# Weight sums as whole units with longer rows, and the last of them begun in the value projection and the first u/z run

## The chip, the cores and the metric

The kernel runs on one core of a Trainium2 chip. The metric is the device time of one execution in microseconds (us); lower is better. The core has a matrix engine (PE, TensorE), a vector engine (DVE), a scalar engine (ACT), a general engine (POOL, GpSimd), and a sync engine (SP) that does nothing but issue transfers. Each engine works through its own instructions in order. Transfers issued by SP go over the hardware DMA queue q1, those issued by POOL over the software queue q0; both run on the same 16 DMA engines.

## What is computed

A decoder trunk of two layers over 512 positions with model width 2048, in float32. Cut to what matters here:

```
h = x @ w_in                          # layer 0: attention and gated convolution
y = concat(y_a, y_b) @ w_out          # 2048 x 2048
x = layer_norm(alpha * x + y)
u, v, z = gelu / gelu / linear of x @ od_w_in      # layer 1: three 2048 x 2048 projections
y = (layer_norm(v) mixed over positions) * u * silu(z)
x = layer_norm(alpha * x + y @ od_w_out)           # 2048 x 2048
```

## The kernel before

**Five runs of seven products.** Behind the attention stand five 2048-wide projections, each done as a block-recursive matrix product with seven block products in place of eight: the layer-0 output projection (called the first output run below), the value projection, two u/z runs (r = 0 and r = 1, each half of the columns of u and of z together), and the layer-1 output projection (the last run). `strassen` runs each; its products are numbered p and come in the order 1, 2, 5, 3, 6, 7, 4. A product has two halves c of its depth and two column groups g; for each (p, g, c) it loads two pages of 512 KB of weights, ACT and DVE split each page into a high and a low part (L85, L86), and PE does 24 matmuls on them (L655 to L657), 96 for each product and 672 for a run.

**Where the weights come from.** Products 1, 2 and 3 use blocks of the weight matrix as they are. Products 5, 7, 6 and 4 need sums of blocks. In the two output runs and the value projection, `chained` keeps eight pages `x` in SBUF, loads them once (SP, L593) and lets POOL add a further block into them by an accumulating transfer (L605), once before each of the products 5, 6 and 4; for p = 7 the sum lies ready in DRAM. In the u/z runs all four sums lie ready in DRAM and SP loads them as `raw` pages (`plain`, L577).

**The sums in DRAM.** `weight_sums` makes them, each by three transfers on POOL's queue: a marker of one element that waits for a given tile and so fixes the earliest time of the step (L227), a copy DRAM to DRAM (L229), and an accumulating copy with rows of 1 KB at most (L233, `max_dma_last_dim=1024`). Each sum is done in two halves d of 512 KB. A step holds two sums (two values of g): 2 MB copied and 2 MB accumulated. There are 2 steps for each of the three chained runs and 8 for each u/z run, in the order 5, 5, 7, 7, 6, 6, 4, 4, where the sum for p = 6 is copied from that for p = 7, and that for 4 from that for 6. Their DRAM tiles are named `ts_` (output runs), `tsv_` (value projection) and `tu_` (u/z).

**Where the steps begin.** The loop over the eight heads h of the attention begins those of the first output run, the value projection and both u/z runs, two and a half for each head:

```
for st in early[5 * h // 2:5 * (h + 1) // 2]:
    st(qT[0:1, 0:1])
```

The two steps of the last run begin at the start of u/z run 0, as soon as the tile `swT` is there (L963). A scheduler places every instruction in its engine's order, so the order of the code is not the order on the engine.

**What else stands in the way of the steps.** In the output runs, POOL also adds the residual into the result tile `xv` (L694) after ACT has put a product there (L692), and DVE then takes its statistics (`ready`, L697). In u/z run 0 SP issues, between the raw pages, loads of scale rows (`row`, L862), loads of `xs` (L886) and stores `xres` (L889), for which DVE works at L873, L874, L887 and L888.

Of the kernel before, what the change touches and what calls it, by code (L numbers as in the profile page):

```python
# [10 lines left out]
F32 = mybir.dt.float32  # L11
F32R = mybir.dt.float32r
AF = mybir.ActivationFunctionType
ALU = mybir.AluOpType
AX = mybir.AxisListType

P = 128
# [48 lines left out]
def trunk(ctx, tc, xT, xn, oneh, cst, table, wa, wv, convw, posT, cw1, cw2, wo0, wuz, wv1, odg, odb, sguw, sgub, wo1, out):  # L66
# [128 lines left out]

    def blocks(w):

        def get(k, n, g, c, d):
            return w[4 * (2 * g + n) + 2 * k + c][:, d * 1024:(d + 1) * 1024]
        return get  # L200

    def uz_blocks(r):

        def get(k, n, g, c, d):
            q, e = 2 * r + g, (2 * k + c) * 512 + d * 256
            return wuz[8 * q + n:8 * q + 8:2, :, e:e + 256].rearrange("i p e -> p i e")
        return get

    def same(t, src):
        return t.rearrange("p (i e) -> p i e", i=4) if len(src.shape) == 3 else t  # L210

    GCS = [(g, c) for c in range(2) for g in range(2)]

    def weight_sums(get, qs, name):


        t = {}
        first = {5: (0, 0), 7: (1, 1)}
        more = {5: (0, 1), 7: (0, 1), 6: (0, 0), 4: (1, 0)}

        def step(q, gcs):
            def run(after):

                for g, c in gcs:
                    for d in range(2):
                        h = t[q, g, c, d] = dram.tile([P, 1024], F32, name=f"{name}{q}{g}{c}{d}")
                        nc.gpsimd.dma_start(h[0:1, 0:1], after)  # L227
                        src = get(*first[q], g, c, d) if q in first else t[{6: 7, 4: 6}[q], g, c, d]
                        nc.gpsimd.dma_start(same(h, src), src)  # L229
                for g, c in gcs:  # L230
                    for d in range(2):
                        src = get(*more[q], g, c, d)
                        nc.gpsimd.dma_start(same(t[q, g, c, d], src), src, accum_op=ALU.add, max_dma_last_dim=1024)  # L233
            return run
        return t, [step(q, GCS[i:i + 2]) for q in qs for i in (0, 2)]

# [1 line left out]
    sumsv, stepsv = weight_sums(blocks(wv1), (7,), "tsv_")  # L238
    sums1, steps1 = weight_sums(blocks(wo1), (7,), "ts1_")
    sumsu, stepsu = zip(*(weight_sums(uz_blocks(r), (5, 7, 6, 4), f"tu{r}_") for r in range(2)))  # L240
    early = steps0 + stepsv + stepsu[0] + stepsu[1]


    with ExitStack() as es:
# [229 lines left out]
        for h in range(NH):  # L474
# [20 lines left out]
            if h == 0:  # L495
                cmp_out(1)
            bz = silu2(ps, "bz")
            for st in early[5 * h // 2:5 * (h + 1) // 2]:
                st(qT[0:1, 0:1])
            t0, tc_ = softmax_branch(h, 0, q, bh, bc)  # L500
            compressed(h, tc_)
# [57 lines left out]
    def in_place(a):  # L559
# [12 lines left out]
            return {1: a(0, 0, c), 2: a(0, 1, c), 5: a(1, 0, c), 3: a(0, 1, c), 7: a(1, 0, c), 6: a(0, 0, c), 4: a(1, 1, c)}[p]  # L572
        return src

    def raw_load(src):
        raw = raw_page()
        nc.sync.dma_start(same(raw, src), src)  # L577
        return raw

    def plain(get, sums):  # L580

        def unit(p, g, c, d):
            return raw_load(sums[p, g, c, d] if p in (5, 7, 6, 4) else get(*{1: (0, 0), 2: (1, 0), 3: (1, 1)}[p], g, c, d))
        return unit

    def chained(get, sums, pool, direct):


        x = {}

        def page(g, c, d):
            x[g, c, d] = pool.tile([P, 1024], F32, tag="x", name="x", bufs=8)
            nc.sync.dma_start(x[g, c, d], get(0, 0, g, c, d))  # L593
            return x[g, c, d]

        def unit(p, g, c, d):
            if p == 1 and c not in direct:
                return page(g, c, d)
            if p in (1, 2, 3):
                if p == 2 and c in direct:  # L600
                    page(g, c, d)
                return raw_load(get(*{1: (0, 0), 2: (1, 0), 3: (1, 1)}[p], g, c, d))
            if p == 7:
                return raw_load(sums[p, g, c, d])
            nc.gpsimd.dma_start(x[g, c, d], get(*{5: (0, 1), 6: (1, 1), 4: (1, 0)}[p], g, c, d), accum_op=ALU.add)  # L605
            return x[g, c, d]
        return unit

# [186 lines left out]
    def done_v(p, g, m, b):  # L795
# [8 lines left out]
            nc.scalar.copy(uv[g, m], b)  # L804
        elif p == 2:
            gelu(0, 0, b)
        elif p == 5:
            nc.scalar.copy(v(1, 1), b)
        elif p == 3:
# [41 lines left out]
    with tc.tile_pool(name="sgu", bufs=2) as sg:  # L851
# [48 lines left out]
        def uz_done(r):  # L900
# [24 lines left out]
            def done(p, g, m, b):  # L925
# [3 lines left out]
                elif p == 2:  # L929
                    u[0, g, m] = tile()  # L930
                    nc.scalar.activation(u[0, g, m], b, AF.Gelu_apprx_tanh)
                    if r == 1 and (g, m) == (1, 1):
                        later.extend(lambda mt=mt, q=q: y_turn(mt, q) for q in range(2) for mt in range(NT))
                elif p == 5:
# [12 lines left out]
                    later.extend([first, lambda: gate(0, g, m)])  # L947
                elif p == 7:
                    add(z[1, g, m], b, ALU.subtract)
                    later.append(lambda: silu(1, g, m))  # L950
                else:
                    u[1, g, m] = tile()
                    nc.vector.tensor_tensor(u[1, g, m], ua[g, m], b, ALU.add)
                    nc.scalar.activation(u[1, g, m], u[1, g, m], AF.Gelu_apprx_tanh)
                    later.append(lambda: gate(1, g, m))
            return done

        for r in range(2):
            for q in (2 * r, 2 * r + 1):
                values(q)  # L960
            for q in (2 * r, 2 * r + 1):
                residual_rows(q)
            for st in steps1 if r == 0 else ():  # L963
                st(swT[0:1, 0, 0:1])
            strassen(sp, x_sums, plain(uz_blocks(r), sumsu[r]), uz_done(r), cuts=True)
        while later:
            drain(1)
# [3 lines left out]
    with tc.tile_pool(name="fin", bufs=1) as fin, tc.tile_pool(name="wx", bufs=1, side="right") as wx:  # L971
# [32 lines left out]
                for i in range(2):  # L1004
                    nc.sync.dma_start(gb[:, i], odg[i:i + 1].to_broadcast([P, DM]))

        strassen(sp, in_place(yT), chained(blocks(wo1), sums1, fin, (0, 1)), take1, by_tile=True, wx=wx)


# [84 lines left out]
```

## Time and profile before

| | |
|---|---|
| median of 3 runs | 1683.38 us (1682.88 to 1684.66) |
| the profiled execution | 1684.09 us, of which its span from the first to the last instruction is 1682.3 us |
| busy in the span: PE, DVE, ACT, POOL | 95%, 58%, 41%, 19% |
| mean granted clock of PE | 0.975 |
| DMA, mean rate | 212 GB/s; q0 took 41.1% of the 16 DMA engines' time, q1 38.5% |
| attention until 780 us | then first output run to 963, value projection to 1120, u/z run 0 to 1320, u/z run 1 to 1485, last run to 1668 us |

The span is the time that the profile's views cut up. A view by windows gives the busy time of an engine in a stretch and, in brackets behind it, how many instructions of the engine ran there. As the clock of PE can fall, the count of matmuls tells more of its progress than its busy time.

### The profile page before, as it was taken

The page shows a single profiled execution, that of the slowest core. Times are in us where ns is not written, and L with a number is a line of the kernel's source. Part 1 is how long each engine was busy: PE and PEld are TensorE (multiplying, and loading weights), DVE is VectorE, ACT ScalarE, POOL GpSimd, SP SyncE. Part 2 cuts the span into 40 slices and gives each one's busy share as a digit, 9 for nine tenths or more (in the row PEclk, how much of TensorE's full clock was granted, in tenths as well). Part 3 has the DMA queues.
Part 4 walks back from the last instruction along what each step waited for, and adds up shares of the span by engine and source line. Part 5 has one row for each costly group of instructions (what it writes and reads, how often), then busy time and mean ns, then how long its engine had stood idle before and what let it go on. Part 6 is the DMA issues. An engine that isn't in the chain of part 4 may idle for free.

```text
span 1682.3 us, 19662 instructions
## 1 busy us (share of the span) xinstructions
PE 1590.3 (95%) x7333; PEld 1318.9 (78%) x7333; DVE 967.5 (58%) x1438; ACT 686.2 (41%) x965; POOL 317.4 (19%) x429
## 2 busy tenths in 40 slices
PE   8899999999999999999789999997799999999895
PEld 6798888888888888887568888875577888877684
DVE  5224443535234444455357985884579855873688
ACT  4123232323233323233335775543455555545441
POOL 0102133333122324133122111131000000002311
PEclk9999999999999999999989999998899999999898
DMA  5548679989859699999999878849975766579962
GB/s 208 192 138 237 170 203 236 236 202 239 194 159 235 166 227 234 217 223 266 277 206 211 271 235 199 190 146 258 280 220 192 242 212 189 173 235 305 229 159 87
DMA packets 157819, 357.44 MB, mean 212 GB/s; under 512 B 15291, under 2 KB 85747, under 8 KB 156444
## 3 DMA queue, kind: packets, MB, share of 16 engines
q0 software_dynamic: 72896, 139.00, 41.1%
q1 hardware_dynamic: 84684, 216.78, 38.5%
q8 instruction: 57, 0.93, 0.2%
q10 hardware_dynamic: 144, 0.41, 0.1%
q14 instruction: 38, 0.31, 0.1%
HBM read 343.51 MB, written 107.52 MB: 268 GB/s over the span
## 4 chain that ended last, share of the span: by engine, by line
PE 78%; DMA 12%; DVE 5%; issue 3%; ACT 1%; POOL 1%; SPq 0%; DVEq 0%; POOLq 0%; ACTq 0%
PE ps L111 12%; PE ps L113 12%; PE ps L112 12%; PE ps L656 11%; PE ps L657 10%; PE ps L655 10%; DMA x<-in_wo_dram 4%; DVE wlo L86 2%; DMA row<-odrow 2%; DMA row<-in_odg_dram 1%; PE ps_t L430 1%; DMA xv<-xres 1%; PE ps L122 1%; DMA xres<-xs 1%; PE ps L121 1%
## 5 line engine op out<-in xcount | busy, mean ns | idle before, releaser
L85 ACT CAST whi<-raw 128x1024 fp32r<-128x1024 f32 (+2 forms) x326 | 337.7, 1036 | 742.0 <-PE ps L112 309.9
L86 DVE TENSOR_TENSOR wlo<-raw,whi 128x1024 fp32r<-128x1024 f32 (+2 forms) x326 | 390.4, 1203 | 429.3 <-ACT whi L85 423.3
L656 PE MATMUL ps<-wlo,shi 128*128 128x512 f32 x1120 | 447.7, 400 | 37.6 <-DVE wlo L86 37.3
L655 PE MATMUL ps<-whi,shi 128*128 128x512 f32 x1120 | 447.4, 402 | 21.4 <-ACT whi L85 20.8
L657 PE MATMUL ps<-whi,slo 128*128 128x512 f32 x1120 | 443.9, 397 | 1.3 <-DVE slo L86 1.3
L111 PE MATMUL ps<-act_hi,whi 128*128 128x512 f32 x864 | 340.6, 394 | 3.8 <-ACT whi L85 3.8
L113 PE MATMUL ps<-act_hi,wlo 128*128 128x512 f32 x864 | 337.7, 391 | 0.0
L112 PE MATMUL ps<-act_lo,whi 128*128 128x512 f32 x864 | 337.5, 391 | 0.0
L656 PEld LDWEIGHTS ps<-wlo,shi 128*128 128x128 f32 x1120 | 215.5, 192 | 92.0 <-DVE wlo L86 46.9
L655 PEld LDWEIGHTS ps<-whi,shi 128*128 128x128 f32 x1120 | 215.1, 192 | 70.4 <-ACT whi L85 23.7
L657 PEld LDWEIGHTS ps<-whi,slo 128*128 128x128 f32 x1120 | 215.2, 192 | 47.5 <-DVE slo L86 2.0
L111 PEld LDWEIGHTS ps<-act_hi,whi 128*128 128x128 f32 x864 | 162.9, 189 | 36.5 <-ACT whi L85 4.0
L113 PEld LDWEIGHTS ps<-act_hi,wlo 128*128 128x128 f32 x864 | 162.7, 188 | 34.9 <-DVE wlo L86 0.8
L112 PEld LDWEIGHTS ps<-act_lo,whi 128*128 128x128 f32 x864 | 162.9, 189 | 32.4
L605 POOL DMA_DIRECT2D x<-in_wo_dram x48 | 42.8, 919 | 445.2 <-DMA raw<-in_wo_dram 322.5
L86 DVE TENSOR_TENSOR wlo<-x,whi 128x1024 fp32r<-128x1024 f32 x80 | 96.9, 1220 | 44.1 <-ACT whi L85 43.5
L233 POOL DMA_DIRECT2D tu<-in_wuz_dram x64 | 75.3, 1188 | 248.1 <-DMA tu<-tu 107.6
L85 ACT CAST whi<-x 128x1024 fp32r<-128x1024 f32 x80 | 83.8, 1050 | 81.7 <-PE ps L657 65.9
L86 DVE TENSOR_TENSOR slo<-y_sb,shi 128x1024 fp32r<-128x1024 f32 x52 | 63.3, 1217 | 0.2 <-ACT shi L85 0.2
L227 POOL DMA_DIRECT2D tu<-qT x64 | 39.7, 843 | 102.1 <-ACT qT L486 101.4
L85 ACT CAST shi<-y_sb 128x1024 fp32r<-128x1024 f32 x52 | 54.7, 1051 | 3.9 <-DVE y_sb L524 1.7
L411 ACT ACTIVATE t_sc<-t_sc,mx 128x128 f32<-128x128 f32 (+1 forms) x64 | 35.1, 550 | 17.3 <-DVE mx L408 17.3
(210 smaller groups left out, 1468.7 us busy)
## 6 DMA issues: line engine op xcount, KB each, us to landing
raw<-in_wa_dram SPq DMA_DIRECT2D x110, 512.0 KB, 6.5
tu<-in_wuz_dram POOLq DMA_DIRECT2D x96, 512.0 KB, 11.0
raw<-tu SPq DMA_DIRECT2D x64, 512.0 KB, 4.1
x<-in_wo_dram POOLq DMA_DIRECT2D x48, 512.0 KB, 10.1
raw<-in_wuz_dram SPq DMA_DIRECT2D x48, 512.0 KB, 5.7
raw<-in_wo_dram SPq DMA_DIRECT2D x44, 512.0 KB, 8.1
ts<-in_wo_dram POOLq DMA_DIRECT2D x32, 512.0 KB, 10.9
tu<-tu POOLq DMA_DIRECT2D x32, 512.0 KB, 9.6
```

The source lines that it names most:

```text
L85: nc.scalar.copy(hi, src)
L86: nc.vector.tensor_tensor(lo, src, hi.bitcast(F32), ALU.subtract)
L111: nc.tensor.matmul(ps, hi[:, w], act_hi[:, kt, :], start=kt == 0, stop=False)
L112: nc.tensor.matmul(ps, hi[:, w], act_lo[:, kt, :], start=False, stop=False)
L113: nc.tensor.matmul(ps, lo[:, w], act_hi[:, kt, :], start=False, stop=kt == KT - 1)
L227: nc.gpsimd.dma_start(h[0:1, 0:1], after)
L233: nc.gpsimd.dma_start(same(t[q, g, c, d], src), src, accum_op=ALU.add, max_dma_last_dim=1024)
L411: nc.scalar.activation(t[:, offs[qb]:offs[qb] + nk], t[:, offs[qb]:offs[qb] + nk], AF.Exp, bias=mx[:, qb:qb + 1], accum_out=sm[:, qb:qb + 1])
L605: nc.gpsimd.dma_start(x[g, c, d], get(*{5: (0, 1), 6: (1, 1), 4: (1, 0)}[p], g, c, d), accum_op=ALU.add)
L655: nc.tensor.matmul(o, s[0][:, k, ms], moving(hi, k), start=new and c == 0 and k == 0, stop=False, **kw)
L656: nc.tensor.matmul(o, s[0][:, k, ms], moving(lo, k), start=False, stop=False, **kw)
L657: nc.tensor.matmul(o, s[1][:, k, ms], moving(hi, k), start=False, stop=c == 1 and k == 3, **kw)
```

## The change

1. The sums are made in whole units of 1 MB: one marker, one copy and one accumulating copy for each, so 132 transfers where there were 264. The accumulating copies may have rows of 2 KB. The copies go in longer pieces (16 pieces of 64 KB for a sum that is copied from a sum).
2. The u/z sums lie in DRAM in the layout of the weight matrix, so SP's loads of them have rows of 1 KB instead of 4 KB.
3. The attention begins 16 steps, two for each head. The last four of u/z run 1 and the two of the last run begin later: those for p = 6 at the end of product 2 of the value projection, those for p = 4 in product 2 of u/z run 0, those of the last run in its product 7.
4. In the last run the half c = 1 of product 1 reads its weights from the pages `x` themselves, as the first output run does, instead of loading them a second time.

```diff
-                    for d in range(2):
-                        h = t[q, g, c, d] = dram.tile([P, 1024], F32, name=f"{name}{q}{g}{c}{d}")
-                        nc.gpsimd.dma_start(h[0:1, 0:1], after)
-                        src = get(*first[q], g, c, d) if q in first else t[{6: 7, 4: 6}[q], g, c, d]
-                        nc.gpsimd.dma_start(same(h, src), src)
+                    src = get(*first[q], g, c) if q in first else t[{6: 7, 4: 6}[q], g, c]
+                    h = t[q, g, c] = dram.tile(list(src.shape), F32, name=f"{name}{q}{g}{c}")
+                    nc.gpsimd.dma_start(h[0:1, 0:1, 0:1] if len(src.shape) == 3 else h[0:1, 0:1], after)
+                    nc.gpsimd.dma_start(h, src)
                 for g, c in gcs:
-                    for d in range(2):
-                        src = get(*more[q], g, c, d)
-                        nc.gpsimd.dma_start(same(t[q, g, c, d], src), src, accum_op=ALU.add, max_dma_last_dim=1024)
+                    nc.gpsimd.dma_start(t[q, g, c], get(*more[q], g, c), accum_op=ALU.add, max_dma_last_dim=2048)
...
-    early = steps0 + stepsv + stepsu[0] + stepsu[1]
+    early = steps0 + stepsv + stepsu[0] + stepsu[1][:4]
...
-            for st in early[5 * h // 2:5 * (h + 1) // 2]:
+            for st in early[2 * h:2 * h + 2]:
                 st(qT[0:1, 0:1])
...
         elif p == 2:
             gelu(0, 0, b)
+            if g and m:
+                stepsu[1][4](v(0, 0)[0:1, 0:1])
+            elif g:
+                stepsu[1][5](v(0, 0)[0:1, 0:1])
...
                     nc.scalar.activation(u[0, g, m], b, AF.Gelu_apprx_tanh)
+                    if m and r == 0:
+                        stepsu[1][6 + g](u[0, g, m][0:1, 0:1])
...
                     add(z[1, g, m], b, ALU.subtract)
+                    if r == 0 and m:
+                        steps1[g](z[1, g, m][0:1, 0:1])
...
-            for st in steps1 if r == 0 else ():
-                st(swT[0:1, 0, 0:1])
...
-        strassen(sp, in_place(yT), chained(blocks(wo1), sums1, fin, (0, 1)), take1, by_tile=True, wx=wx)
+        strassen(sp, in_place(yT), chained(blocks(wo1), sums1, fin, (0,)), take1, by_tile=True, wx=wx)
```

Line numbers of the changed kernel are a few lower or higher: the marker stands at L228, the copy at L229, the accumulating copy at L231, the addition into `x` at L606, that into `xv` at L695.

**POOL where the attention ends, before.** The last copies and accumulations of head 7's steps (for p = 4 of u/z run 1) stand ahead of the first addition into a page `x` of the first output run.

```order
L233 DMA tu_4010_5680<-in_wuz_dram 512x1x256 [waits DMASW7_49]
L229 DMA tu_4011_5683<-tu_6011_5651 16x8192 [waits DMASW4_49,DMASW0_49]
L229 DMA tu_4110_5686<-tu_6110_5654 16x8192 [waits DMASW5_49,DMASW1_49]
L229 DMA tu_4111_5689<-tu_6111_5657 16x8192 [waits DMASW6_49,DMASW2_49]
L233 DMA tu_4011_5683<-in_wuz_dram 512x1x256 [waits DMASW4_49]
L233 DMA tu_4110_5686<-in_wuz_dram 512x1x256 [waits DMASW5_49]
L233 DMA tu_4111_5689<-in_wuz_dram 512x1x256 [waits DMASW6_49]
L605 DMA x<-in_wo_dram 128x1024 [waits DMAHW4_49,PE_49]
L605 DMA x<-in_wo_dram 128x1024 [waits DMAHW0_49,DMASW3_49,DVE_49]
```

**The same place of POOL in the changed kernel.** Head 7's two steps are now those for p = 7 of u/z run 1 (`tu_7`).

```order
L228 DMA tu_711_5499<-qT 1x1 [waits DMASW1_49]
L606 DMA x<-in_wo_dram 128x1024 [waits DMAHW4_49,PE_49]
L229 DMA tu_700_5488<-in_wuz_dram 512x1x512 [waits DMASW6_49]
L229 DMA tu_710_5491<-in_wuz_dram 512x1x512 [waits DMASW7_49,DMASW4_49]
L231 DMA tu_700_5488<-in_wuz_dram 512x1x512 [waits DMASW5_49,DMASW3_49]
L231 DMA tu_710_5491<-in_wuz_dram 512x1x512 [waits DMASW4_49]
L229 DMA tu_701_5496<-in_wuz_dram 512x1x512 [waits DMASW0_49]
L229 DMA tu_711_5499<-in_wuz_dram 512x1x512 [waits DMASW1_49]
L231 DMA tu_701_5496<-in_wuz_dram 512x1x512 [waits DMASW7_49]
L231 DMA tu_711_5499<-in_wuz_dram 512x1x512 [waits DMASW2_49,DMASW0_49]
L695 DMA xv<-in_xn_dram 128x512 [waits DVE_49,PE_49,Activation_49]
```

One addition into `x`, which waits for a page that SP can load only when the attention has ended (DMAHW4 is that load), now stands ahead of all copies and accumulations of head 7's steps; the other additions into `x` for product 5 stand behind the four of `xv` that follow.

**POOL in product 5 of the value projection, changed kernel.** Before, only additions into `x` stand here, eight in a row for product 6.

```order
L606 DMA x<-in_wv_dram 128x1024 [waits DMASW2_49,DVE_49]
L229 DMA tu_601_7604<-tu_701_5496 16x16384 [waits DMASW3_49,DMASW0_49]
L229 DMA tu_611_7607<-tu_711_5499 16x16384 [waits DMASW4_49,DMASW1_49]
L231 DMA tu_601_7604<-in_wuz_dram 512x1x512 [waits DMASW5_49,DMASW3_49]
L231 DMA tu_611_7607<-in_wuz_dram 512x1x512 [waits DMASW6_49,DMASW4_49]
L228 DMA tu_600_7626<-xv 1x1 [waits DMASW7_49,Activation_49]
L606 DMA x<-in_wv_dram 128x1024 [waits DVE_49]
L229 DMA tu_600_7626<-tu_700_5488 16x16384 [waits DMASW7_49,DMASW2_49]
L229 DMA tu_610_7629<-tu_710_5491 16x16384 [waits DMASW0_49]
L231 DMA tu_600_7626<-in_wuz_dram 512x1x512 [waits DMASW2_49]
L231 DMA tu_610_7629<-in_wuz_dram 512x1x512 [waits DMASW5_49,DMASW3_49]
L606 DMA x<-in_wv_dram 128x1024 [waits DMASW6_49,DVE_49]
```

Two steps (for p = 6 of u/z run 1) have come among them: the first three additions for product 6 stand ahead of the copies, the fourth between the steps, and the last four behind both.

**POOL in u/z run 0, changed kernel.** Before, the only steps here are the two of the last run (`ts_`), with their markers at the run's start. The markers named `<-uz` wait for tiles that product 2 (Activation) or product 7 (DVE) writes.

```order
L231 DMA tu_400_8800<-in_wuz_dram 512x1x512 [waits DMASW4_49]
L231 DMA tu_410_8803<-in_wuz_dram 512x1x512 [waits DMASW5_49]
L228 DMA tu_401_8861<-uz 1x1 [waits Activation_49]
L228 DMA tu_411_8864<-uz 1x1
L228 DMA ts_700_9529<-uz 1x1 [waits DVE_49]
L228 DMA ts_710_9532<-uz 1x1
L228 DMA ts_701_9581<-uz 1x1 [waits DVE_49]
L229 DMA tu_401_8861<-tu_601_7604 16x16384 [waits DMASW0_49]
L229 DMA tu_411_8864<-tu_611_7607 16x16384 [waits DMASW6_49,DMASW1_49]
L231 DMA tu_401_8861<-in_wuz_dram 512x1x512 [waits DMASW7_49,DMASW5_49]
L231 DMA tu_411_8864<-in_wuz_dram 512x1x512 [waits DMASW6_49]
L229 DMA ts_700_9529<-in_wo_dram 16x16384 [waits DMASW2_49]
```

The first step for p = 4 (`tu_400`, `tu_410`) runs alone after product 2. The second has its markers issued then, but its copies stand behind markers of the last run that wait for product 7.

## Rows read from the trace of the kernel before

**Rows 1.** PE by windows: length, busy (count), granted clock, DMA share, GB/s.

```profile
300.00:770.00 470.00, 470.00 (x2305) 1.00 0.87 212
780.00:834.00 54.00, 47.77 (x194) 0.97 1.08 298
834.00:872.00 38.00, 25.58 (x97) 0.82 0.98 183
963.00:1120.40 157.40, 156.14 (x705) 1.00 0.74 191
1060.00:1080.00 20.00, 20.00 (x90) 1.00 0.82 168
1120.40:1191.00 70.60, 49.93 (x192) 0.85 1.04 259
1191.00:1243.00 52.00, 47.10 (x194) 0.93 0.82 259
1322.00:1485.40 163.40, 163.40 (x747) 1.00 0.61 193
1492.00:1543.00 51.00, 49.11 (x196) 0.91 1.01 304
1543.00:1576.00 33.00, 26.39 (x99) 0.84 1.00 218
```

**Rows 2.** DMA queues from 600 to 770: packets, MB, share of 16 engines.

```profile
q0 software_dynamic: 14895, 24.27, 70.1%
q1 hardware_dynamic: 3888, 13.90, 23.9%
```

**Rows 3.** DMA queues from 812 to 832, in the first output run.

```profile
q0 software_dynamic: 750, 2.74, 68.8%
q1 hardware_dynamic: 750, 2.74, 36.6%
```

**Rows 4.** DMA queues from 1119 to 1191, the start of u/z run 0.

```profile
q0 software_dynamic: 5630, 8.39, 55.6%
q1 hardware_dynamic: 8321, 10.26, 47.8%
```

**Rows 5.** Chain of waits, 770 to 862: start, length, what.

```profile
777.65 0.33 SPq L593
...
780.40 16.61 DMA x<-in_wo_dram
...
797.57 18.64 DMA x<-in_wo_dram
...
846.04 7.47 DMA xv<-in_xn_dram
```

**Rows 6.** POOL in order of time at the same place: start, length, idle before.

```profile
789.76 1.15 POOL L233 DMA_DIRECT2D tu<-in_wuz_dram  x1 [1.10 <-DMA tu<-tu]
797.57 2.75 POOL L605 DMA_DIRECT2D x<-in_wo_dram  x3 [6.66 <-DMA x<-in_wo_dram]
```

**Rows 7.** POOL in the value projection, in order of time.

```profile
1007.41 0.85 POOL L605 DMA_DIRECT2D x<-in_wv_dram  x1 [26.98 <-DVE wlo L86]
...
1026.00 0.85 POOL L605 DMA_DIRECT2D x<-in_wv_dram  x1 [1.42 <-DVE wlo L86]
```

**Rows 8.** Chain of waits in u/z run 0, 1120 to 1200.

```profile
1130.42 14.34 DMA row<-odrow
...
1151.22 10.78 DMA row<-in_odg_dram
...
1164.55 9.20 DMA xres<-xs
```

**Rows 9.** DMA issues of the whole execution: count, KB each, median us to landing.

```profile
raw<-tu SPq DMA_DIRECT2D x64, 512.0 KB, 4.1
...
raw<-in_wuz_dram SPq DMA_DIRECT2D x48, 512.0 KB, 5.7
```

**Rows 10.** DMA queue q0 from 860 to 868, when accumulating transfers into SBUF run alone.

```profile
q0 software_dynamic: 404, 1.49, 103.3%
```

More of the change, by code (lines that the diff above doesn't have):

```diff
@@ L196, in blocks, with uz_blocks, get, half @@
     def blocks(w):
-        def get(k, n, g, c, d):
-            return w[4 * (2 * g + n) + 2 * k + c][:, d * 1024:(d + 1) * 1024]
-        return get
[L202 to L210, printed above, removed]
+        return lambda k, n, g, c: w[4 * (2 * g + n) + 2 * k + c]
+    def uz_blocks(r):
+        def get(k, n, g, c):
+            q, e = 2 * r + g, (2 * k + c) * 512
+            return wuz[8 * q + n:8 * q + 8:2, :, e:e + 512]
+        return get
+    def half(unit, d):
+        if len(unit.shape) == 3:
+            return unit[:, :, d * 256:(d + 1) * 256].rearrange("i p e -> p i e")
+        return unit[:, d * 1024:(d + 1) * 1024]
     GCS = [(g, c) for c in range(2) for g in range(2)]
@@ L573, in in_place, with same @@
         return src
+    def same(t, src):
+        return t.rearrange("p (i e) -> p i e", i=4) if len(src.shape) == 3 else t
     def raw_load(src):
@@ L582, in unit @@
         def unit(p, g, c, d):
-            return raw_load(sums[p, g, c, d] if p in (5, 7, 6, 4) else get(*{1: (0, 0), 2: (1, 0), 3: (1, 1)}[p], g, c, d))
+            return raw_load(half(sums[p, g, c] if p in (5, 7, 6, 4) else get(*{1: (0, 0), 2: (1, 0), 3: (1, 1)}[p], g, c), d))
         return unit
@@ L592, in page @@
             x[g, c, d] = pool.tile([P, 1024], F32, tag="x", name="x", bufs=8)
-            nc.sync.dma_start(x[g, c, d], get(0, 0, g, c, d))
+            nc.sync.dma_start(x[g, c, d], half(get(0, 0, g, c), d))
             return x[g, c, d]
@@ L601, in unit @@
                     page(g, c, d)
-                return raw_load(get(*{1: (0, 0), 2: (1, 0), 3: (1, 1)}[p], g, c, d))
+                return raw_load(half(get(*{1: (0, 0), 2: (1, 0), 3: (1, 1)}[p], g, c), d))
             if p == 7:
-                return raw_load(sums[p, g, c, d])
-            nc.gpsimd.dma_start(x[g, c, d], get(*{5: (0, 1), 6: (1, 1), 4: (1, 0)}[p], g, c, d), accum_op=ALU.add)
+                return raw_load(half(sums[p, g, c], d))
+            nc.gpsimd.dma_start(x[g, c, d], half(get(*{5: (0, 1), 6: (1, 1), 4: (1, 0)}[p], g, c), d), accum_op=ALU.add)
             return x[g, c, d]
```

## The prediction

> **What bounds the kernel now.** I read the windows of PE first. From 1060 to 1080 us 90 matmuls fill 20 us, so one takes 0.222 us at the full clock [rows 1]. A product of 96 then takes 21.3 us, and the 1 MB (1.05 million bytes) of weights for 24 matmuls must come every 5.33 us, 197 GB/s. Counts at this price tell what each stretch loses. The attention loses nothing: PE is busy 470.00 of 470 us. The value projection loses 157.4 - 705 x 0.222 = 0.9 us, and u/z run 1 shows no idle time at all. The losses lie in three places: products 1 and 2 of the first output run (54.0 - 194 x 0.222 = 10.9) and its product 5 (38.0 - 97 x 0.222 = 16.4); u/z run 0 up to 1191 (70.6 - 42.7 = 27.9) and the two products behind (52.0 - 43.1 = 8.9); products 1 and 2 of the last run (51.0 - 43.6 = 7.4) and its product 5 (33.0 - 22.0 = 11.0) [rows 1]. In these stretches the DMA engines are at a share of about 1, and the clock falls to between 0.82 and 0.97 of full speed after the waits. So PE bounds the kernel except where weights arrive late, and there the DMA does.
>
> Second, the queues. In the attention q0, that is the sums, takes 70.1% of the DMA engines and q1 only 23.9% [rows 2], and PE feels nothing, as each unit of weights there feeds 48 matmuls. In the first output run q0 and q1 move the same number of packets, 750 each, in 20 us, of 4 KB on either side [rows 3]: q1 brings 137 GB/s where 197 are needed. That is the loss in product 2.
>
> Third, the chain of waits. At 780 it runs through a load of a page x that takes 16.61 us, then the addition into it, 18.64 us, issued at 797.57 right when the load has landed [rows 5, 6]. In u/z run 0 it runs through row loads and stores one behind another (14.34, 10.78, 9.20 us, [rows 8]) while the last run's sums, 8.39 MB in q0, hold 55.6% of the engines [rows 4].
>
> **The change, part by part.** Its sum is made against the profiled execution (1684.09 us, 0.7 over the median 1683.38); I add it to the median.
>
> *Half as many transfers on POOL.* POOL is busy 19% of the span and PE waits for none of its issues in the attention, so 132 fewer are worth nothing by themselves. What a step moves stays the same: 2 MB copied, 2 MB accumulated. Its price in DMA time: 24.27 MB at 70.1% of 170 us is 4.9 us of all 16 engines for each million bytes [rows 2], 20.6 us for a step of 4.19; the run's start gives 55.6% of 72 us for 8.39, 20.0 for a step [rows 4]. Longer rows may lower it: additions with rows of 4 KB run alone at 1.49 MB in 8 us, 186 GB/s [rows 10], a rate that a step's mixture of copies and accumulations (4.19 MB in 20.6 us, 204 GB/s) already reaches. I take no gain; the bound is a tenth, 2 us for a step.
>
> *Head 7's steps and the start of the first output run.* POOL's order is the point here. Before, the last accumulation of the sums is issued at 789.76, and the additions into x follow at 797.57 [rows 6]. Now one addition into x stands ahead of all copies of head 7's two steps and waits for the page that SP loads only after 777.65 [rows 5]. POOL sits idle over it for most of head 7; then 8.39 MB of sums, 41 us of all engines, begin at about 788 (797 at the latest, when that page landed before) and stand ahead of the seven other additions for product 5. Product 2 is better off: against additions of 4 KB a packet it had equal counts; against rows of 2 KB it gets about two thirds of the bytes, some 200 GB/s, so I give it 8 of its 10.9 us back (bounds 0 and 10.9). Until its loads are done, at about 826, q0 gets 0.65 of the engines, 25 of the 41 us; the other 16 end at 842; four additions into xv (1.05 MB, 5 us) and a page x (0.52 MB, 2.8 us by [rows 10]) make 850. The last page lands at 867, so product 5, which PE reaches at 826, ends at about 877 with some us for the clock: 51 us where it took 38, +13. Together **+5**, between -8 (pages in time for product 5 as before) and +20 (first addition at 797, the pages late by as much as the 18.64 us of [rows 5]).
>
> *Two steps in the value projection.* They stand among the additions for product 6, which were issued at 1007.41 to 1026.00 [rows 7]. Product 6 is the fifth of the run: 963 + 4 x 22.5 = 1053. So there are 27 us and more of slack. The two steps take 41 us of engines from about 1013; the last four additions, for its second half, are issued near 1050 and land near 1066, where that half begins at 1064. Product 3 loads its raw pages meanwhile, 4 KB a packet. I take **+3**, between 0 and +12 (the second half waits for both steps).
>
> *U/z run 0 without sums at its start.* The products after 1191 have the same row loads and stores with q0 empty and lose 8.9 us, so of the 27.9 some 19 are the two steps' price, 9.5 each: **-19** (bounds -10, if the chain of row loads is the larger part, and -24).
>
> *Four steps later in it.* The first for p = 4 runs alone in product 5. The second cannot: its copies stand behind markers that wait for product 7, so it and the two of the last run all start where product 4 starts, 61 us of engines, and run on into u/z run 1. There PE needs 197 GB/s, and the DMA share is 0.61 with no sums [rows 1], so the 0.4 that is left would need 150 us to hide them; the steps are not spread so. Loads of sums now have rows of 1 KB too: 5.7 us to landing instead of 4.1 [rows 9], hidden by the four pages loaded ahead (10.7 us of PE) unless the queues are full; then it is part of the step's price. At 9.5 a step this is +38; at nothing, 0. As two of the four meet fewer row loads I take 8 each, **+32**, with bounds of 8 and 40.
>
> By the Trainium skill (DMA: Bandwidth & Descriptors, Queues, rings and completion order) each DMA engine goes round-robin between queues at packet granularity. The equal 750 and 750 agree. By this rule longer pieces on q0 take more of the engine from raw pages of 1 KB, which speaks for a price of 8 or more; were it shared by bytes, 5 a step would do and the sum would be 12 lower.
>
> *The last run.* Four raw loads fall away, 2.1 MB, some 7 us at the 304 GB/s of its first window [rows 1], where 7.4 us are lost; product 5's 11.0 come later. **-5**, between -10 and 0.
>
> The sum: +5 +3 -19 +32 -5 = **+16**, 1683.4 + 16 = **1699 us**.
>
> **Rivals.**
> *The sums are hidden where they go (faster).* u/z run 0 gets its 19 us back and pays 2 a step, -11; the first output run keeps product 2's gain and loses nothing in product 5, -8; the last run -5: -24, **1659 us**. For it: u/z run 1 and the value projection have DMA time free (0.61, 0.74). Against it: POOL's order bunches three steps. It decides at about 4 us a step: below that the u/z part is a gain. By the Trainium skill (the same page, Anatomy of one DMA) each transfer on POOL's path costs some 2 us beside its bytes; no row here separates that part, and by the rule alone half as many transfers would shorten each step and bring this case. Chance 0.28.
> *Loss moved, not changed.* The steps cost 4 to 5 each and the rest cancels: within 3 us of **1683**. Chance 0.10.
> *The value projection stalls (slower still).* If the last four additions for product 6 land 12 us late and those for product 4 slip behind them, +12 in place of +3 and the clock falls: **1710**. Against it: 27 us of slack. Chance 0.12, and the forecast itself 0.50.
>
> **How the numbers follow.** From no change, about 0.2% (3.4 us) can be told. Forecast and stall are slower, 0.62; the middle case is the same, 0.10; the rival is faster, 0.28. The range reaches down to the faster rival's near side, 1662, and up past the stall with part of +20 in the first output run, 1722; the forecast's own range is 1688 to 1715.
>
> **What would show it.** Right: POOL idle from head 7 until about 787, then copies of tu; product 5 of the first output run longer than 38 us with waits for x; u/z run 0 up to its second product under 55 us; then waits of PE for whi and wlo from its product 4 into u/z run 1, raw pages landing after 10 us and more. Wrong: no idle PE there, or a product 5 no longer than before. The forecast fails first if a step costs under 4 us where it now stands.

## The result, and the profile after

The changed kernel takes 1821.54 us (median of 4 runs, 1819.90 to 1823.00) where the kernel before takes 1684.02 (4 runs, 1682.88 to 1687.89). The ratio is 1.0812, with a 95% interval of 1.0791 to 1.0833: slower by 137 us. The forecast was slower by 16, and 1821 lies far outside its range, 1662 to 1722. The profiled execution spans 1817.7 us, against 1682.3 before.

Where the time went is read from the windows of PE in the changed kernel: the stretch, its length, PE's busy time and its number of matmuls, the granted clock, the DMA share and GB/s. They answer to [rows 1].

```profile
300.00:770.00 470.00, 461.61 (x2239) 1.00 0.67 172
791.60:840.00 48.40, 44.09 (x192) 1.00 0.92 290
840.00:915.00 75.00, 26.36 (x96) 0.64 0.86 162
1010.50:1209.10 198.60, 163.01 (x705) 0.91 0.76 193
1102.00:1160.00 58.00, 26.29 (x98) 0.71 0.86 171
1209.10:1408.50 199.40, 171.49 (x697) 0.92 0.76 229
1408.50:1624.90 216.40, 178.59 (x755) 0.91 0.68 199
1631.00:1802.30 171.30, 161.15 (x676) 0.96 0.78 203
```

Four stretches pay. In the attention PE is idle for 8.4 us of these 470, where it was busy for all of them before, and the attention ends at 791.6 instead of 780. Product 5 of the first output run takes 75.0 us where it took 38.0. The value projection takes 198.6 us in place of 157.4, and 58.0 of them are its product 6, which needs 22. U/z run 0 is as long as before (199.4 against 200), and u/z run 1, with the gap ahead of it, takes 216.4 in place of 165. Only the last run is shorter: its 676 matmuls are done in 171 us and not in 176. In the stretches behind the attention the mean granted clock is 0.64 to 0.96 of the full 2.4 GHz (the lower level is 1.2), and PE comes out of long waits there. So the matmuls behind a wait are dearer too: the 96 of product 5 of the first output run keep PE busy for 26.4 us, where 96 take 21.3 at the full clock.

The waits of PE say the same (who waited for whom: us in all, times, the longest).

```profile
PE ps L656 <- ACT whi L85: 104.7, 11, 48.0
PE ps L657 <- DVE wlo L86: 40.5, 26, 13.0
...
PE ps_s L390 <- ACT qT L484: 7.6, 4, 1.9
```

The last row was not there before, and it is nearly all of the 8.4 us: in four heads ACT writes `qT` directly ahead of its use, in an order of ACT in which it stands behind another tile (`bz`). Why the scheduler put it there is not shown.

Look now at the DMA issues of the page (count, KB each, median us from issue to landing). Before, raw pages took 4.1 and 5.7 us [rows 9]; those rows are little changed here. What is new is the first row.

```profile
tu<-in_wuz_dram POOLq DMA_DIRECT2D x48, 1024.0 KB, 31.3
raw<-tu SPq DMA_DIRECT2D x64, 512.0 KB, 4.6
x<-in_wo_dram POOLq DMA_DIRECT2D x48, 512.0 KB, 15.4
...
x<-in_wv_dram POOLq DMA_DIRECT2D x24, 512.0 KB, 17.4
```

Copies and additions from the weights into the u/z sums take 31.3 us (median). Before, with half the bytes, they took 11.0, so twice that or less was to be expected of a full queue, and these are issued two by two. Yet the DMA engines were not full: from 600 to 770 the queues of the changed kernel show (packets, MB, share of 16 engines)

```profile
q0 software_dynamic: 21056, 16.90, 46.9%
q1 hardware_dynamic: 3846, 13.72, 24.8%
```

The sums fall behind while more than a quarter of the DMA engines' time is free. The 24.27 MB and 70.1% of [rows 2] are no measure for this: the change begins two steps a head in place of two and a half. The same stretch of e6 below, with the same places and no loss in the attention, has

```profile
q0 software_dynamic: 7718, 18.89, 50.6%
```

So the low share alone does not show the fault; that it goes with late landings does. And POOL's order does the rest. Its issues at the first output run, in order of time (start, length of the issue, what; in brackets the idle time before, and what ended it), answer to [rows 6]:

```profile
750.33 3.77 POOL L228 DMA_DIRECT2D tu<-qT  x4
800.42 0.92 POOL L606 DMA_DIRECT2D x<-in_wo_dram  x1 [46.32 <-DMA x<-in_wo_dram]
801.10 2.49 POOL L229 DMA_DIRECT2D tu<-in_wuz_dram  x2
820.20 1.91 POOL L231 DMA_DIRECT2D tu<-in_wuz_dram  x1 [16.62 <-DMA tu<-in_wuz_dram]
...
856.25 3.86 POOL L231 DMA_DIRECT2D tu<-in_wuz_dram  x2 [29.27 <-DMA tu<-in_wuz_dram]
...
881.61 0.86 POOL L606 DMA_DIRECT2D x<-in_wo_dram  x1 [16.14 <-DMA tu<-in_wuz_dram]
```

That is the picture the prediction drew, POOL idle behind one addition into `x` and then head 7's two steps, only that the two take 80 us and more (801 to 881, when POOL is released by one of their last additions) instead of 41, with the other additions for product 5 behind them.

### The profile page after: what moved, and what is told of

It is laid out like the page before. It is cut to its first block, busy times and chain, and to the rows that moved or that the text cites. A ratio compares the mean times of both kernels' runs of the same rounds, so it can differ in the third digit from the quotient of the medians.

```text
span 1817.7 us, 19456 instructions
## 1 busy us (share of the span) xinstructions
PE 1611.6 (89%) x7333; PEld 1326.1 (73%) x7333; DVE 970.3 (53%) x1438; ACT 686.6 (38%) x965; POOL 242.9 (13%) x297
## 4 chain that ended last, share of the span: by engine, by line
PE 60%; DMA 20%; DVE 9%; issue 8%; POOL 2%; ACT 1%; SPq 1%; DVEq 0%; POOLq 0%; ACTq 0%
PE ps L111 11%; PE ps L112 11%; PE ps L113 11%; PE ps L657 6%; PE ps L658 6%; PE ps L656 6%; DMA x<-in_wo_dram 4%; DVE wlo L86 3%; DMA xs<-xhat 3%; DMA raw<-in_wuz_dram 3%; DMA tu<-xv 2%; DMA xres<-xs 2%; DMA x<-in_wv_dram 2%; ACT whi L85 1%; DMA tu<-in_wuz_dram 1%
## 5 line engine op out<-in xcount | busy, mean ns | idle before, releaser
L86 DVE TENSOR_TENSOR wlo<-raw,whi 128x1024 fp32r<-128x1024 f32 (+2 forms) x322 | 385.6, 1203 | 486.5 <-ACT whi L85 480.6
L85 ACT CAST whi<-raw 128x1024 fp32r<-128x1024 f32 (+2 forms) x322 | 333.4, 1036 | 768.8 <-PE ps L112 317.2
L657 PE MATMUL ps<-wlo,shi 128*128 128x512 f32 x1120 | 454.0, 406 | 40.7 <-DVE wlo L86 40.5
L86 DVE TENSOR_TENSOR wlo<-x,whi 128x1024 fp32r<-128x1024 f32 x84 | 101.8, 1222 | 82.8 <-ACT whi L85 81.6
L85 ACT CAST whi<-x 128x1024 fp32r<-128x1024 f32 x84 | 88.0, 1051 | 151.0 <-DMA x<-in_wo_dram 62.6
L231 POOL DMA_DIRECT2D tu<-in_wuz_dram x32 | 61.8, 2019 | 297.5 <-DMA tu<-in_wuz_dram 174.9
L606 POOL DMA_DIRECT2D x<-in_wo_dram x48 | 46.3, 1041 | 310.0 <-DMA x<-in_wo_dram 222.9
L698 DVE BATCH_NORM_STATS2 stats<-xv 128x6 f32<-128x512 f32 x32 | 22.1, 689 | 59.7 <-DMA xv<-in_xn_dram 46.1
## 6 DMA issues: line engine op xcount, KB each, us to landing
tu<-in_wuz_dram POOLq DMA_DIRECT2D x48, 1024.0 KB, 31.3
```

What stands on the lines that cost most here:

```text
L85: nc.scalar.copy(hi, src)
L86: nc.vector.tensor_tensor(lo, src, hi.bitcast(F32), ALU.subtract)
L231: nc.gpsimd.dma_start(t[q, g, c], get(*more[q], g, c), accum_op=ALU.add, max_dma_last_dim=2048)
L606: nc.gpsimd.dma_start(x[g, c, d], half(get(*{5: (0, 1), 6: (1, 1), 4: (1, 0)}[p], g, c), d), accum_op=ALU.add)
L657: nc.tensor.matmul(o, s[0][:, k, ms], moving(lo, k), start=False, stop=False, **kw)
L698: nc.vector.bn_stats(stats[:, 2 * t + m, 2 * g + n], at(t, m, g, n))
```

## The experiments

The theory formed on this is the **layout theory**. Before, a transfer into a u/z sum was described with 128 rows outermost; the change makes the sum `[4, 128, 512]`, so that 4 slices stand outermost, and by the theory the DMA engines that share such a transfer are then few. Its rivals are the **places theory** (the later places of the last steps cost the time) and the **units theory** (pieces of 1 MB with rows of 2 KB crowd the queues). Ratios below are each to runs of the kernel before on the same chip, and "us" worked out from a ratio takes 1684 us as one.

| kernel | layout of a u/z transfer | units | places | direct columns | median us | ratio (95%) |
|---|---|---|---|---|---|---|
| changed | 4 outermost | whole | new | one | 1821.54 | 1.0812 (1.0791 to 1.0833) |
| e1 | 128 outermost, in memory too | whole | new | one | 1703.30 | 1.0111 (1.0091 to 1.0130) |
| e6 | 128 outermost, memory as changed | whole | new | one | 1705.42 | 1.0124 (1.0110 to 1.0139) |
| e3 | 128 outermost | halves | new | one | 1706.04 | 1.0131 (1.0117 to 1.0146) |
| e2 | 4 outermost | halves | old | two | 1854.90 | 1.1032 (1.0999 to 1.1066) |
| e5 | 4 outermost | whole | old | one | 1849.84 | 1.0989 (1.0964 to 1.1014) |
| e9 | 128 outermost | whole | old | one | 1679.31 | 0.9964 (0.9951 to 0.9976) |
| e4 | 128 outermost | halves | old | one | 1680.11 | 0.9963 (0.9949 to 0.9977) |

**e1, the layout undone.**

```diff
+    def rows(src):
+        return src.rearrange("i p e -> p i e") if len(src.shape) == 3 else src
-  src = get(*first[q], g, c) if q in first else ...
+  src = rows(get(*first[q], g, c)) if q in first else ...
   h = t[q, g, c] = dram.tile(list(src.shape), F32, ...)
-  nc.gpsimd.dma_start(t[q, g, c], get(*more[q], g, c), accum_op=ALU.add, max_dma_last_dim=2048)
+  nc.gpsimd.dma_start(t[q, g, c], rows(get(*more[q], g, c)), accum_op=ALU.add, max_dma_last_dim=2048)
```

SP's loads of the sums follow the new layout; that part of the edit is left out here.

> The changed kernel, with one thing put back: the u/z sums stand in DRAM with their 128 rows outermost (row by row 4 pieces of 2 KB) instead of 4 slices of 128 rows; units, row length of the additions (2 KB), places and the last run stay as changed. Layout theory (with 4 slices outermost a transfer into a u/z sum is carried by few of the 16 DMA engines, so 1 MB lands in about 31 us): the additions into tu land in 8 to 15 us, the attention ends at 780 to 783 instead of 792, product 5 of the first output run and product 6 of the value projection lose their 30 and 40 us, and the time falls by 100 to 150 us, to 1670 to 1715. Places theory (the last steps at later places cost the time): nothing changes there, 1800 to 1825. Units theory (whole units of 1 MB with 2 KB rows hold the queue and crowd out the other one): nothing changes there either, 1800 to 1825.

1703.3 us. All but 19 us of the 137 are gone with places and units as changed; neither rival allows that.

**e2, the layout alone.** The kernel before with `h = dram.tile([4, P, 256])` for a half u/z sum, and copy and addition described as `[4, 128, 256]`.

> The kernel before, with one thing changed: the half units of the u/z sums stand in DRAM as 4 slices of 128 rows of 1 KB; same bytes, same number of transfers, same pieces of 1 KB, same places. Layout theory: the transfers of 512 KB into tu go from about 11 us to landing to 16 us or more, the sums no longer fit under the attention, and the time rises by 50 to 200 us, to 1735 to 1885. Places theory and units theory: 1680 to 1690, no change.

1854.9 us, slower by 10.3%: the layout alone, with pieces, bytes and places of before, costs 174 us. A transfer of 512 KB now takes 18.0 us to land, and the waits of PE show where the sums no longer fit:

```profile
PE ps_s L389 <- ACT qT L483: 95.6, 5, 51.7
PE ps L655 <- ACT whi L85: 94.8, 8, 36.9
```

The first is the sums' queue at work: in one head ACT waits 49.7 us with its next `qT` until markers that read the last one have come through POOL.

```profile
735.26 0.60 ACT L483 ACTIVATE qT<-ps 128x512 f32<-128x512 f32 x1 [49.70 <-DMA tu<-qT]
```

**e3, the places (and the one direct column) alone.** The kernel before with the loop `early[2 * h:2 * h + 2]`, the four calls of `stepsu` and `steps1` in `done_v` and `done`, and `(0,)`, as in the diff of the change.

> The kernel before in its half units and its layout, with the changed places of the last steps and the last run's one direct column. Layout theory: the loss of 137 us is not here; what is left is what the prediction summed for the places, 1683 + 16 = 1699, between 1662 and 1722. Places theory: 1790 to 1825. Units theory: 1680 to 1700.

1706.04 us. The places are not the 137 us; with the one direct column they cost 22, near the forecast's 16.

**e5, whole units and 4 outermost at the old places.** The changed kernel with `early[5 * h // 2:5 * (h + 1) // 2]`, all steps of `stepsu[1]` in it and `steps1` at the start of u/z run 0.

> The changed kernel (whole units, 4 slices outermost, 2 KB rows, one direct column) with all steps at the places of before: 20 early ones in the attention, two of the last run at the start of u/z run 0. Layout theory: all 16 u/z steps, each with two additions of 31 us side by side, and copies of 18 us ahead of them, need some 16 x 50 = 800 us where the attention offers 530, so the sums run on into the output run and the value projection: 1780 to 1900, and the loss lies there and not in u/z run 1. Places theory: back to 1680 to 1690. Units theory: 1780 to 1830.

1849.84 us. The attention ends at 872.7 and the first output run takes 266.7 us; u/z run 1 has no idle time. With this layout the new places are even the better ones (1821); they take four steps out of the attention, which there ends at 791.6.

**e6, only the order of description turned.** The layout in memory, the units, the rows of 2 KB and the places stay those of the change; the transfer is walked row by row (`rows` is the helper of e1). The copies from sum to sum are turned with it.

```diff
-  nc.gpsimd.dma_start(h, src)
+  nc.gpsimd.dma_start(rows(h), rows(src))
-  nc.gpsimd.dma_start(t[q, g, c], get(*more[q], g, c), accum_op=ALU.add, ...)
+  nc.gpsimd.dma_start(rows(t[q, g, c]), rows(get(*more[q], g, c)), accum_op=ALU.add, ...)
```

> The changed kernel with the same layout in DRAM (4 slices of 128 rows of 2 KB), the same units, bytes, pieces and places; only the order in which a transfer into a u/z sum is described is turned, 128 rows outermost and 4 slices inside, on both sides. Theory of the outermost count (the 4 that stands first in the description decides how many DMA engines share the transfer): additions into tu land in 10 to 15 us, time 1690 to 1715, as with the layout of 128 rows outermost. Theory of the memory layout (slices far apart, or both sides in the same stripes, are slow by their addresses): additions still land in about 30 us, time 1800 to 1825.

1705.42 us. The same bytes at the same addresses land in 12.9 us:

```profile
tu<-in_wuz_dram POOLq DMA_DIRECT2D x48, 1024.0 KB, 12.9
```

So it is not where the data lies but what stands first in the description; 0.0688 of the time, 116 us, hang on it. A second thing came back with it. Head 7's steps are again issued inside the attention, ahead of every addition into `x`:

```profile
749.13 1.27 POOL L234 DMA_DIRECT2D tu<-in_wuz_dram  x1 [15.39 <-DMA tu<-in_wuz_dram]
789.32 6.15 POOL L609 DMA_DIRECT2D x<-in_wo_dram  x7 [36.19 <-DMA x<-in_wo_dram]
```

The addition that stood ahead of them in the changed kernel came with the description, not with the places: the scheduler's order on POOL changed with it. The 116 us hold both, the slow transfers and this order; e12 below has the transfers alone. What the places do with good transfers is read from the windows of this kernel, one for each run:

```profile
780.40:950.40 170.00, 161.47 (x705) 0.98 0.95 244
950.40:1121.60 171.20, 159.49 (x705) 0.98 0.86 224
1121.60:1324.40 202.80, 172.57 (x698) 0.92 0.84 242
1324.40:1509.80 185.40, 170.23 (x754) 0.97 0.71 214
1516.00:1687.50 171.50, 162.89 (x676) 0.95 0.79 203
```

Against before (182.9, 157.4, 200.0, 165.0, 175.6) that is -12.9, +13.8, +2.8, +20.4 and -4.1 us.

**e12, the transfers by themselves.** Nothing of the kernel is computed. Twice round, each behind the landing of the last:

```python
both("four", wuz[n:n + 8:2, :, 0:512], wuz[n:n + 8:2, :, 512:1024])              # [4, 128, 512]
both("eight", wuz[n:n + 16:2, 0:64, 0:512], wuz[n:n + 16:2, 0:64, 512:1024])     # [8, 64, 512]
...
```

with "two" `[2, 128, 512]` (512 KB), "sixteen" `[16, 32, 512]` and "rows" `[128, 4, 512]`; `both` writes a marker (L78), copies (L79) and adds (L80).

> The transfers by themselves: nothing of the kernel is computed (the output is zeros); one after another, each behind the landing of the last, a copy and then an accumulating copy between places in DRAM, in rows of 2 KB, described with 2 slices outermost (512 KB), and with 4, 8, 16 slices and with 128 rows outermost (1 MB each), twice round. Theory of the outermost count (so many DMA engines share the transfer, up to 16): the time to landing halves from 4 to 8 and again from 8 to 16, to within some fixed 2 us: additions about 30 (4), 16 (8), 9 (16), 9 (128 rows), and 2 slices with half the bytes about 30 again. Rival (only the case of 128 rows, whose pieces lie in address order, is fast): 4, 8 and 16 take about the same 30 us. Rival (a transfer alone is fast and the 30 us come from the other queue beside it): all about 9 us.

POOL's issues in order of time: an L80 stands where the copy before it has landed, and the marker of the next name where the addition has.

```profile
18.56 1.94 POOL L80 DMA_DIRECT2D two<-in_wuz_dram  x1 [12.22 <-DMA two<-in_wuz_dram]
43.62 0.56 POOL L78 DMA_DIRECT2D four<-two  x1 [23.12 <-DMA two<-in_wuz_dram]
...
59.59 1.93 POOL L80 DMA_DIRECT2D four<-in_wuz_dram  x1 [13.02 <-DMA four<-in_wuz_dram]
84.90 0.57 POOL L78 DMA_DIRECT2D eight<-four  x1 [23.38 <-DMA four<-in_wuz_dram]
...
95.94 1.39 POOL L80 DMA_DIRECT2D eight<-in_wuz_dram  x1 [8.34 <-DMA eight<-in_wuz_dram]
110.39 0.56 POOL L78 DMA_DIRECT2D sixteen<-eight  x1 [13.06 <-DMA eight<-in_wuz_dram]
...
120.54 1.07 POOL L80 DMA_DIRECT2D sixteen<-in_wuz_dram  x1 [7.65 <-DMA sixteen<-in_wuz_dram]
131.07 0.55 POOL L78 DMA_DIRECT2D rows<-sixteen  x1 [9.46 <-DMA sixteen<-in_wuz_dram]
...
139.38 1.18 POOL L80 DMA_DIRECT2D rows<-in_wuz_dram  x1 [5.64 <-DMA rows<-in_wuz_dram]
149.50 0.54 POOL L78 DMA_DIRECT2D two<-rows  x1 [8.94 <-DMA rows<-in_wuz_dram]
```

From an L80 to the next marker an addition of 1 MB takes 25.3 us with 4 outermost, 14.5 with 8, 10.5 with 16 and 10.1 with 128 rows; with 2 and half the bytes 25.1. The second round agrees within 0.6 us. From 4 to 8 it falls by 10.8 us and to 16 by 4.0, where a pure halving would give 5.4. Neither rival allows this: 4, 8 and 16 differ, and a transfer with 4 is slow with no other queue beside it. The windows in the middle of these five additions show the cause itself in the DMA share, which is a mean over 16 engines (length, busy time of DVE and POOL, clock, DMA share, GB/s):

```profile
22.00:42.00 20.00, 0.00 (x0) 0.00 (x0) 1.00 0.17 25
62.00:82.00 20.00, 0.00 (x0) 0.00 (x0) 1.00 0.31 48
99.00:109.00 10.00, 0.00 (x0) 0.00 (x0) 1.00 0.55 98
124.00:130.00 6.00, 0.00 (x0) 0.00 (x0) 1.00 0.95 147
143.00:149.00 6.00, 0.00 (x0) 0.00 (x0) 1.00 0.85 148
```

0.17, 0.31 and 0.55 are a little over 2, 4 and 8 sixteenths. The packets in these windows agree: of those of 2 KB, which carry the data, mostly 2 or 3 are in flight at a time with 2 outermost, 4 or 5 with 4 and 8 or 9 with 8. One takes some 185 ns there and with 128 rows (210 with 16), so no packet is slower; fewer run side by side. Part of the little over is packets of 8 bytes, many with 2 and 4 outermost, which take 0.03 to 0.04 of the share there. With 4 slices outermost a quarter of the DMA engines does the work. The Trainium skill (DMA: Bandwidth & Descriptors, Why a DMA increments its semaphore by 16 and not by 1) states this as a rule: the number of engines is the largest up to 16 that divides the size of the slowest dimension, other than 1, on both sides. Every row here agrees.

**e4, the one direct column alone.** The kernel before with `(0,)` in place of `(0, 1)` in the last run.

> The kernel before with only the last run's one direct column in place of two. The term of the prediction for it alone: -5 us, between -10 and 0, so 1674 to 1684 (ratio about 0.997), with the last run at 170 us instead of 175.5. Rival (the gain of the last run comes from the sums being done elsewhere, not from the loads that fall away): no change, 1683 to 1685.

Ratio 0.9963 (0.9949 to 0.9977), 6 us faster, between 4 and 9. The last run's products 1 and 2 take 44 us in place of 51; its product 5 takes 33.0 us as before.

**e9, whole units at the old places**, with the turned description: e5 with the edit of e6.

> The changed kernel with the turned description (128 rows outermost), and all steps at the places of before: what is left of the change is whole units, rows of 2 KB in the additions, half as many transfers, and the one direct column. Term of the prediction for the units (nothing): the same as the kernel before with one direct column alone, 1676 to 1683. Rival (fewer transfers or longer rows shorten a step by a tenth or more): the sums are done earlier at the first output run, 1664 to 1674. Rival (longer rows crowd out the raw loads): 1686 to 1700.

Ratio 0.9964, the same as e4 with its halves. Half as many transfers, rows of 2 KB in the additions and rows of 1 KB in SP's loads are together worth no time that can be measured, at the new places neither (e1 and e6 against e3). The sums' engine time did fall: for their 139 MB q0 took 41.1% of 1676 us in e4 and 38.3% of 1678 in e9, while q1 took 38.7% in both.

**e7, the value projection's two steps later.** On e6:

```diff
-            if g and m:
-                stepsu[1][4](v(0, 0)[0:1, 0:1])
-            elif g:
-                stepsu[1][5](v(0, 0)[0:1, 0:1])
...
         elif p == 7:
             add(v(1, 1), b, ALU.subtract)
             gelu(1, 1)
+            if m:
+                stepsu[1][4 + g](v(1, 1)[0:1, 0:1])
```

> The kernel of the turned description, with the two steps in the value projection begun at its product 7 instead of product 2, behind all 24 additions into x. Theory of the queue (the 12 us that the value projection lost with balanced sums come from the steps' transfers standing ahead of the additions for products 6 and 4): the run goes from 170 back to 158 to 161 us; the two steps then run from about 1080 to 1125, where the queue of the sums was idle; time 1688 to 1698 if the start of u/z run 0 takes 0 to 5 us of it. Rival (the steps cost their DMA time wherever they stand): 1700 to 1710, the loss moved to u/z run 0.

Ratio 1.0109 (1.0092 to 1.0127), as before the edit. The windows of the value projection and of u/z run 0 in this kernel:

```profile
949.80:1107.30 157.50, 156.24 (x705) 1.00 0.82 209
1107.30:1323.80 216.50, 178.18 (x697) 0.91 0.89 252
```

The value projection is back at its 157.5 us, 13.7 less than in e6, so the queue theory holds for it; u/z run 0 has taken on 13.7, so the rival holds for the sum. The second step's additions are issued at 1119 and 1122, when u/z run 0 with its row loads has begun.

**e8, the other four one by one.** On e7, `stepsu[1][6]` and `[7]` at products 3 and 7 of u/z run 0, `steps1` at products 2 and 3 of u/z run 1.

> As the one before, and the four remaining steps spread one by one: those for product 4 of u/z run 1 at products 3 and 7 of u/z run 0, those of the last run at products 2 and 3 of u/z run 1. Bunching theory (three steps that start together at the end of u/z run 0 take 60 us of one queue and so the first product of u/z run 1 waits; one step at a time hides): u/z run 0 with 185 to 195 us, u/z run 1 with 164 to 170 us, time 1662 to 1680, faster than before. Rival (a step costs 8 us wherever it runs beside a product of u/z): 1690 to 1700.

1692.69 us, ratio 1.0045 (1.0029 to 1.0060). 11 us come back, where the bunching theory wanted 25 to 43; the time lies in the rival's range. U/z run 1 takes 187.3 us (1303.2 to 1490.5) with the tail of one step and two whole ones beside it, 22 over its 165: between 7 us a step, with the tail counted as one, and 11. This is the fastest of 12 executions, 1685.68. Bunching is a part; a step beside a u/z product is not free even alone.

**e10 and e11, places taken from these readings.** e10 is e9 with the last run's steps moved from u/z run 0's start to product 6 of the value projection; e11 is e10 with three steps a head (the last two lines of the diff).

```diff
-            for st in steps1 if r == 0 else ():
-                st(swT[0:1, 0, 0:1])
...
         elif p == 6:
             add(uv[g, m], b)
+            if g:
+                steps1[m](uv[g, m][0:1, 0:1])
...
-            for st in early[5 * h // 2:5 * (h + 1) // 2]:
+            for st in early[3 * h:3 * h + 3]:
```

> As the one before, and the last run's two steps begun at product 6 of the value projection, behind all its additions into x, instead of at the start of u/z run 0. From the runs so far: the start of u/z run 0 gets back the 19 us that the sums take there; a first step at the value projection's end was hidden, a second cost some 15 as it ran into u/z run 0, and these begin 18 us earlier: 0 to 8 us lost. 1658 to 1672. Rival (no free place; a step costs 6 us or more wherever it stands): 1672 to 1682.

> As the one before, with three steps a head in the attention in place of two and three by turns, so that none is left for head 7. With the sums done before the first output run its products 1, 2 and 5 lose 11 to 13 us less, as in the runs with two a head; 1645 to 1661. Rival (three steps, about 60 us of one queue, do not fit beside a head and hold up the attention): the attention ends 5 us or more later than 780, 1662 or more.

e10 takes 1660.33 us, ratio 0.9853 (0.9838 to 0.9868), and e11 1649.27, ratio 0.9785 (0.9770 to 0.9800). Both are faster than the kernel before and the changed one, each inside the time expected. The windows of e11, one for each run:

```profile
778.20:947.60 169.40, 161.48 (x705) 0.98 0.96 246
947.40:1107.80 160.40, 157.06 (x706) 1.00 0.89 227
1108.00:1288.00 180.00, 163.98 (x696) 0.99 0.76 233
1288.00:1452.90 164.90, 164.90 (x754) 1.00 0.62 193
1460.00:1630.10 170.10, 161.85 (x674) 0.97 0.79 205
```

U/z run 0 is 20 us shorter than before, the first output run 13.5, and u/z run 1 has no idle time; the value projection pays 3.0 for the two steps at its end. The attention ends at 778, so three steps a head fit beside it.

## Why the prediction was wrong

The direction was right, by a mechanism that the prediction did not have. The 137 us split into 116 for the description (changed against e6: 1.0812 - 1.0124), 27 for the places (e6 against e9, 0.0160; e3 against e4, 0.0168), -6 for the direct column (e4) and 0 for the units (e9 against e4). The split hangs on the order in which the parts are taken: at the old places the description costs 173 (e5 against e9), and the new places then give 30 back (changed against e5).

**The step that failed** is the first of the change: "What a step moves stays the same", and with it the price, 20 us of all 16 DMA engines for each step. The bytes stayed, the description did not. The change named the new layout only for SP's loads (its point 2), but the tile takes its shape from the weights, and the copies and additions are described in it too. The price was worked out from a mean over 16 engines [rows 2], which held only as long as all 16 shared each transfer. A u/z step now takes 40 us or more (two of them 80, as shown above), each of its transfers from the weights on a quarter of the engines, and later additions and markers in the same queue stand behind it; that is why the loss shows in four stretches, the attention among them, to which the prediction gave nothing. POOL's order, as shown ahead of the prediction, names a u/z transfer `512x1x256` before and `512x1x512` after; the number that changed, what stands outermost, is not in that name.

**Head 7 and the first output run, +5.** As told for the changed kernel: POOL idle until 800 (forecast 788, 797 at the latest), then head 7's copies, then product 5 late. That product lost 37 us and not 13, as the two steps took twice their price. For the places alone the sign was wrong: with good transfers the steps are issued in the attention (e6), and the run gains 12.9: some 6 in products 1 and 2, where 8 was taken, and 7.0 in product 5, where 13 were to be lost.

**The value projection, +3.** With good transfers it loses 13.8, which is the rival that the value projection stalls (+12, given a chance of 0.12). "27 us of slack" failed: the additions of the second half stand behind both steps, and product 6 waits. e7 shows it by setting the steps behind them.

**U/z run 0, -19, and the later steps, +32.** Measured together +23.2 for +13 (e6). Taking the steps from its start gives 24.7 us in that run, at the bound named, -24 (u/z run 0 in e9, then in e10):

```profile
1114.20:1318.40 204.20, 172.46 (x698) 0.93 0.82 238
1118.10:1297.60 179.50, 167.43 (x698) 0.96 0.77 234
```

Against that 179.5 the four later steps of e6 cost 23.3 in u/z run 0 (202.8), and 20.4 in u/z run 1, some 44 in all: an estimate of 11 each, where 8 was taken and 40 was the bound for the four. Three of them bunched, as told; spread in e8 they cost 11 less.

**The last run, -5.** Measured -6 (4 to 9), in its products 1 and 2.

**Units, 0.** Measured 0. With the page's rule on a transfer's fixed cost (the Trainium skill, DMA: Bandwidth & Descriptors, Anatomy of one DMA) half as many transfers would have shortened the steps; e9 and e4 show no such gain in time, though q0's engine time fell by some 7%, within the tenth named as bound. That the queue has bytes to move in between is a possible reason, and was not tried.

Without the new description the sum, 1699, would have come near a measured 1705 (e6), but by luck: three of its terms were off by 10 to 18 us, one of them the other way.

## What to carry to other kernels

When a transfer's shape changes, ask first what stands outermost in its description, on both sides: with 2, 4 or 8 there on both sides, as tried here, that many DMA engines carried it, and everything behind it in its queue waited. A DMA share well under 1 while transfers land late is the sign: the share is a mean over 16 engines, and 0.25 can be four of them full. Transfers that run beside a stretch bound by loads cost it their time; here the free places, or nearly so, were the attention and the tail of the value projection, not the gaps that the mean shares of the u/z runs seemed to offer.

## What was not expected of the hardware

Turning the order of a description, with no byte moved to another address, took the transfers of 1 MB into the u/z sums from 31.3 us (median) to 12.9 in the kernel (e6). Alone, where the target's layout was turned too, an accumulating one went from 25.3 to 10.1 (e12). The issue on POOL changes with it: 1.93 us with 4 outermost, 1.39 with 8, 1.07 with 16 and 1.18 with 128 rows, for the same bytes in the same rows of 2 KB.
